# Reordering how the first right operands of a two-layer hybrid trunk are prepared on one Trainium2 core

## The chip, the cores and the metric

One core of a Trainium2 chip runs one program. The metric is device time in microseconds (us) of one execution. The engines are named as the profile names them: PE (TensorE matmuls), PEld (its weight loads), DVE (VectorE), ACT (ScalarE), POOL (GpSimd), SP (SyncE, which issues the DMA transfers here).

## The reference, cut to what matters

Two layers act on a latent stream `x` (512 tokens) and a context `s` (256 tokens), both of width 1024, float32. A layer is a half-step SwiGLU feed-forward (FFN), a token mixing (neighbourhood attention beside a two-way recurrent scan), and a second half-step FFN. The change touches only what precedes the first FFN of layer 0:

```python
mx = jnp.split((silu_c @ w_mod[l] + b_mod[l])[:, None, :], N_MOD, axis=-1)   # nine modulations; ms likewise
x = x + 0.5 * mx[2] * swiglu(modulate(rms_norm(x, norm_gain[l, 0]), mx[0], mx[1]), ffn_up[l, 0], ffn_down[l, 0])
# rms_norm: x * rsqrt(mean(x*x) + eps) * gain;  modulate: x * (1 + scale) + shift
# swiglu: (silu(gate) * up) @ w_down, with gate, up = split(x @ w_up)
```

## The kernel before

**Layout.** Both streams lie side by side, transposed: eight tiles `x[k]` of 128 channels by 768 tokens (512 latent, 256 context). A matrix product takes a 128x128 weight block on the left and a token block on the right. Every float32 operand is split in two, `hi` (rounded, made by ACT) and `lo` (the rest, made by DVE as source minus `hi`), and a product is the three matmuls hi·hi, hi·lo, lo·hi (`split`, line 201).

**The up projection.** `up` (line 372) computes each of 22 column blocks `f` of the FFN's first matrix by a Strassen-Winograd scheme: seven products instead of eight, each of four k-tiles with three matmuls, so 84 matmuls (line 394) in a block. The right operands are seven combinations of the four quarters of the scaled input. They are made once for an FFN and used by all 22 blocks. The norm's factor `rstd` is applied after the products; the shifts of the modulation ride along as four extra columns of products 2 to 6. The seven products of a block take the PSUM banks "a", "co", "g", "p", "g", "p", "g" in that order (there are two of "a", one of "co").

**Making the right operands.** `prep_wino(kt)` (line 258) handles the k-tiles `kt` and `kt+4`. It scales both into `xs0`, `xs1` (ACT, by `gs`, latent and context columns apart), splits the left half of each as products 0 and 1, makes two differences on POOL and splits product 5, makes one more on POOL, splits products 2, 3 and 4, makes the last difference on DVE and splits product 6. Then `squares` (line 223) adds x² of the two tiles into `acc`: ACT squares into a tile `sq`, DVE adds. So one k-tile pair has 4 scalings, 7 splits, 3 subtractions on POOL, 1 on DVE, 2 squares. In layer 0's first FFN the shifts are not known yet, so `shifts=False`: the four edge columns are copied away (`edge`, line 281), and `prep_shifts` fills the shift columns of products 2 to 6 later, k-tile by k-tile, 20 small splits.

**The start of the program** (`run`, line 1173): load and multiply modulation 1, which gives `gs`; load `x`; load the weights `raw` of block 0; then for each of four k: `prep_wino(k)` and one step of modulation 0 (`mod`, line 177: a 1 MB load and 8 x 4 matmuls in bank "g"); then `prep_shifts`. The FFN begins with `prep_end` (line 312): it reduces `acc` over channels on PE (`ssps`, bank "a"), takes the root on ACT and the reciprocal on DVE, spreads the result by PE (`rsps`, twice bank "a") and copies it to `rstd`. Fillers (modulations 2, 4 and 3, in bank "a") are emitted between the blocks.

**What sets the order.** Nothing is ordered by hand here. A planner (`schedule_with_timeline_sim=True`) gives each engine a fixed order: an instruction has a priority by its place in the program, and a later one that is ready in the planner's own timing goes ahead of an earlier one that is not. Tiles come from tags with a counted number of buffers (`TAGS`, line 60): "g3" has three, "q4" three, "z" three, "x" six. The split parts of the right operands borrow the buffers of many tags in the order of `PARTS` (line 65): the iterator `operand_parts` (line 247) hands out half tiles, 56 in all. `wq`, the split weights of products 0, 1, 3 and 5, also lives in "q4"; `acc` and `rstd` in "z"; `sq` and the FFN's work tiles `up_g`, `up_u` in "g3". The scaled `xs` lie in "x" for k = 0 to 2 and in "g3" for k = 3.

Of the kernel before, what the change touches and what calls it, by code (L numbers as in the profile page):

```python
# [11 lines left out]
AF = mybir.ActivationFunctionType  # L12
ALU = mybir.AluOpType
# [13 lines left out]
XH = T // 2 + 2  # L27
LAT, CTX = slice(0, NL), slice(NL, T)
# [27 lines left out]
def free_ap(ap, dims, offset=0):  # L56
    return bass.AP(tensor=ap.tensor, offset=ap.offset + offset, ap=[list(ap.ap[0])] + [list(d) for d in dims])
# [5 lines left out]


PARTS = ("st",) * 3 + ("k",) * 2 + ("sp",) * 8 + ("ob",) * 4 + ("q4",) + ("z",) * 2 + ("x",) * 6 + ("r",) * 2
PARTS_LAT = ("st",) + PARTS[3:]

BANKS = dict(g=2, ch=1, co=1, p=2, a=2)
# [29 lines left out]
def interleave(gen, filler):  # L98
    for n, _ in enumerate(gen):
        for _ in range(5 if n < 2 else 1):  # L100
            next(filler, None)
    for _ in filler:
        pass
# [6 lines left out]
class Net:  # L110
# [135 lines left out]

    def operand_parts(self):
        h = self.half(self.prep_ctx)
        for tag in PARTS if self.prep_ctx else PARTS_LAT:
            t = self.t(tag, "b", dt=F32R)  # L250
            for o in range(0, TAGS[tag][0] - h + 1, h):
                yield t[:, o:o + h]
# [2 lines left out]
    def half(ctx):  # L255
        return XH if ctx else NL // 2 + 2

    def prep_wino(self, kt, tag="g3", shifts=True):

        l, s = self.prep_key  # L260
        h = self.half(self.prep_ctx)
        n = h if shifts else h - 4
        x0, x1 = [self.t(tag, f"xs{i}", 2 * XH) for i in range(2)]
        for k, t in ((kt, x0), (kt + 4, x1)):
            for xs, j in ((LAT, 0), (CTX, 1))[:2 if self.prep_ctx else 1]:
                self.act(t[:, xs], self.x[k][:, xs], AF.Copy, scale=self.gs[l, s][:, k, j:j + 1])
            if shifts:
                self.act(t[:, 2 * h - 4:2 * h].rearrange("p (a c) -> p a c", a=2), free_ap(self.mods[l][:, 3 * s, k], [[0, 2], [1, 2]]), AF.Copy)
        a, b = slice(0, h), slice(h, 2 * h)

        def part(i, src):
            hi, lo = next(self.parts)[:, 0:h], next(self.parts)[:, 0:h]
            w = src.shape[-1]
            self.split(src, hi[:, 0:w], lo[:, 0:w])
            self.bs[i].append((hi, lo))

        part(0, x0[:, a])
        part(1, x1[:, a])
        if not shifts:
            for i, t in enumerate((x0, x1)):  # L280
                self.nc.gpsimd.tensor_copy(self.edge[:, i, kt], t[:, n:h])
            a, b = slice(0, n), slice(h, h + n)
        self.tt(x0[:, a], x0[:, b], x0[:, a], ALU.subtract, self.nc.gpsimd)
        self.tt(x0[:, b], x1[:, b], x0[:, b], ALU.subtract, self.nc.gpsimd)
        part(5, x1[:, b])
        self.tt(x1[:, b], x1[:, b], x0[:, a], ALU.subtract, self.nc.gpsimd)
        part(2, x1[:, b])
        part(3, x0[:, b])
        part(4, x0[:, a])
        self.tt(x1[:, a], x1[:, b], x1[:, a], ALU.subtract)  # L290
        part(6, x1[:, a])
        self.squares(kt)
        self.squares(kt + 4)

    def prep_shifts(self):

        l, s = self.prep_key
        h = self.half(self.prep_ctx)
        n = h - 4
        e0, e1 = [self.edge[:, i].rearrange("p k (a c) -> p k a c", a=2) for i in range(2)]  # L300
        s0, s1 = [free_ap(self.mods[l][:, 3 * s, k], [[2, 4], [0, 2], [1, 2]]) for k in (0, 4)]
        c = {i: self.ends[:, j].rearrange("p k (a c) -> p k a c", a=2) for j, i in enumerate((2, 3, 4, 6))}
        self.tt(c[4], s0, e0, ALU.subtract)
        self.tt(c[3], s1, s0, ALU.subtract)
        self.tt(c[2], s1, c[4], ALU.subtract)
        self.tt(c[6], c[2], e1, ALU.subtract)
        c[5] = s1
        for i in (2, 3, 4, 5, 6):
            for k in range(4):
                hi, lo = [t[:, n:h].rearrange("p (a c) -> p a c", a=2) for t in self.bs[i][k]]  # L310
                self.split(c[i][:, k], hi, lo)
# [861 lines left out]
    def run(self, out):  # L1173
        nc = self.nc
        self.x = [self.t("r", f"x{k}", T) for k in range(KD)]
        for _ in self.mod(0, 1, "st", SW, "a"):
            pass
        for k in range(4):
            for m in (k, k + 4):
                nc.sync.dma_start(out=self.x[m], in_=self.a["x"][:, m])  # L1180
        self.prep_begin(0, 0, True)
        edge = self.t("ro", "edge", 96).rearrange("p (i k n) -> p i k n", k=4, n=4)
        self.edge, self.ends = edge[:, 0:2], edge[:, 2:6]
        steps = self.mod(0, 0, "st", SW, "g")
        for k in range(4):
            self.prep_wino(k, "x" if k < 3 else "g3", False)
            next(steps, None)
        for _ in steps:
            pass
        self.prep_shifts()  # L1190
        mods = self.fillers([(0, i) for i in (2, 4, 3)], "ro", 256, "a")
        for l in range(L):
            last = l == L - 1
            self.xd = self.dp.tile([KD, 128, T], F32, name=f"xd{l}")

            def to_mix(m):
                if m == 0:
                    self.prep_begin(l, 1, True)
                for k in (m, m + 4):
                    self.prep(k)  # L1200
                    self.spill(k)

            def to_ffn(m):
                if m == 0:
                    self.prep_begin(l, 2, not last)
                self.prep_wino(m)

            def onward(m):
                if last:
                    for k in (m, m + 4):  # L1210
                        nc.sync.dma_start(out=out[:, k], in_=self.x[k][:, LAT])
                    return
                if m == 0:
                    self.prep_begin(l + 1, 0, True)
                self.prep_wino(m)

            interleave(self.ffn(l, 0, True, to_mix), mods)
            self.mix(l, last, to_ffn)
            interleave(self.ffn(l, 1, not last, onward), iter(()))
# [100 lines left out]
```

## Time and profile before

| | us |
|---|---|
| median of 3 runs | 3880.44 |
| the three runs | 3858.85, 3880.44, 3891.4 |
| the profiled execution | 3867.65 |
| its span, first to last instruction | 3865.8 |
| PE busy in the span | 3593.8 (93%) |
| DVE busy | 2918.1 (75%) |
| ACT busy | 1503.8 (39%) |
| POOL busy | 1078.3 (28%) |

The profile is of one execution, recorded by the hardware; its own time stands beside its span, and the difference is what lies around the span. The share of busy time is an average over stages with different limits. The busy time of DVE and POOL includes time in which an instruction has begun and is held up. The granted clock is the share of TensorE's full clock (2.4 GHz) that was granted; 0.5 is the lower of its two levels.

### The profile page before, as it was taken

How to read it: one execution, taken by the hardware profiler on the slowest of the kernel's cores; microseconds unless marked ns; L12 is line 12 of the kernel's file. 1: busy time of each engine (PE TensorE's matmuls, PEld its weight loads, DVE VectorE, ACT ScalarE, POOL GpSimd, SP SyncE). 2: the span in 40 equal slices, each digit the busy share in tenths (PEclk: the TensorE clock that was granted, in tenths of full speed). 3: DMA queues.
4: the chain of work that ended last, by engine and by line, in shares of the span. 5: the costliest groups of instructions: out<-in, count | busy, mean ns of one | idle time of the engine just before them, and what ended most of it. 6: DMA issues, size and time to landing. Idle time of an engine off the chain costs nothing. (4 is left out here: it accounts for less than half of the span.)

```text
span 3865.8 us, 73287 instructions
## 1 busy us (share of the span) xinstructions
PE 3593.8 (93%) x28980; PEld 3116.1 (81%) x28980; DVE 2918.1 (75%) x5612; ACT 1503.8 (39%) x2996; POOL 1078.3 (28%) x1208
## 2 busy tenths in 40 slices
PE   6999999999899899899998999999999996879999
PEld 4789998787665667799998999998786665768999
DVE  6578786666777776888888888886668677667878
ACT  5233334334343433433335333334434343244433
POOL 3222230202222211322233222230203123124665
PEclk9999999999798799899998999999999895789999
DMA  5321113322345263112211111213333431221232
GB/s 205 122 86 66 69 63 101 99 92 79 98 139 160 74 194 96 36 66 72 76 69 47 66 66 66 76 63 113 105 101 121 147 97 33 76 66 66 88 108 79
DMA packets 213943, 352.50 MB, mean 91 GB/s; under 512 B 46432, under 2 KB 128992, under 8 KB 201312
## 3 DMA queue, kind: packets, MB, share of 16 engines
q1 hardware_dynamic: 213600, 347.81, 27.7%
q8 instruction: 229, 3.75, 0.4%
q14 instruction: 114, 0.93, 0.1%
HBM read 305.26 MB, written 42.47 MB: 90 GB/s over the span
## 5 line engine op out<-in xcount | busy, mean ns | idle before, releaser
L394 PE MATMUL mw<-b,wq 128*128 128x386 f32 (+1 forms) x4224 | 788.6, 329 | 18.4 <-DVE wq L165 13.3
L394 PEld LDWEIGHTS mw<-b,wq 128*128 128x128 f32 x4224 | 705.0, 191 | 38.8 <-DVE wq L165 17.7
L352 PE MATMUL mm<-h,whi 128*128 128x256 f32 (+1 forms) x2816 | 650.1, 326 | 2.8 <-ACT h L171 1.8
L394 PE MATMUL mw<-b,whi 128*128 128x386 f32 (+1 forms) x2112 | 518.6, 328 | 14.9 <-DVE b L165 8.3
L168 DVE SCALAR_TENSOR_TENSOR x<-mm,mods,x 128x256 f32<-128x256 f32 (+1 forms) x704 | 390.7, 581 | 184.8 <-PE mm L352 181.3
L352 PEld LDWEIGHTS mm<-h,whi 128*128 128x128 f32 x2816 | 465.8, 188 | 58.4 <-issue 8.9
L352 PE MATMUL mm<-h,wlo 128*128 128x256 f32 (+1 forms) x1408 | 439.8, 325 | 2.0 <-DVE wlo L165 1.9
L394 PEld LDWEIGHTS mw<-b,whi 128*128 128x128 f32 x2112 | 374.3, 191 | 20.6 <-DVE b L165 10.5
L171 ACT ACTIVATE whi<-wraw 128x512 fp32r<-128x512 f32 x312 | 195.9, 629 | 490.1 <-PE mm L352 274.2
L165 DVE TENSOR_TENSOR wq<-raw,wq 128x512 fp32r<-128x512 f32 x352 | 312.8, 891 | 55.7 <-ACT wq L171 53.4
L394 PE MATMUL mw<-b,wlo 128*128 128x386 f32 (+1 forms) x1056 | 347.0, 329 | 3.6 <-DVE wlo L165 2.7
L171 ACT ACTIVATE wq<-raw 128x512 fp32r<-128x512 f32 x352 | 220.1, 629 | 303.7 <-PE mw L394 284.7
L352 PEld LDWEIGHTS mm<-h,wlo 128*128 128x128 f32 x1408 | 261.6, 188 | 27.9 <-DVE wlo L165 2.6
L165 DVE TENSOR_TENSOR up_g<-up_g,mw 128x386 f32<-128x386 f32 (+1 forms) x352 | 181.9, 517 | 78.8 <-PE mw L394 69.1
L165 POOL TENSOR_TENSOR raw<-raw,s 128x512 f32<-128x512 f32 x88 | 122.0, 1386 | 400.3 <-DVE wq L165 396.5
L165 DVE TENSOR_TENSOR wlo<-wraw,whi 128x512 fp32r<-128x512 f32 x268 | 186.3, 696 | 51.5 <-ACT whi L171 34.9
L171 ACT ACTIVATE whi<-s 128x512 fp32r<-128x512 f32 x176 | 110.1, 628 | 281.5 <-PE mm L352 199.2
L165 POOL TENSOR_TENSOR s<-raw 128x512 f32<-128x512 f32 x88 | 127.6, 1450 | 304.7 <-DVE wlo L165 293.9
L352 PE MATMUL mm<-x,whi 128*128 128x258 f32 (+2 forms) x832 | 209.2, 337 | 0.1
L394 PEld LDWEIGHTS mw<-b,wlo 128*128 128x128 f32 x1056 | 201.4, 191 | 7.6 <-DVE wlo L165 7.1
L165 POOL TENSOR_TENSOR up_g<-up_g,rstd 128x386 f32<-128x386 f32 (+1 forms) x88 | 107.0, 1216 | 346.6 <-DVE up_g L165 346.6
L188 PE MATMUL modps<-wmod,cs 128*32 128x256 f32 x1152 | 164.8, 443 | 28.1 <-DMA wmod<-in_w_mod_dram 27.3
(249 smaller groups left out, 7090.9 us busy)
## 6 DMA issues: line engine op xcount, KB each, us to landing
raw<-in_ffn_up_dram SPq DMA_DIRECT2D x88, 1024.0 KB, 5.2
wmod<-in_w_mod_dram SPq DMA_DIRECT2D x208, 256.0 KB, 3.0
wraw<-in_ffn_down_dram SPq DMA_DIRECT2D x176, 256.0 KB, 3.1
wraw<-in_w_in_dram SPq DMA_DIRECT2D x104, 256.0 KB, 2.9
wmod<-in_w_mod_dram SPq DMA_DIRECT2D x96, 128.0 KB, 2.3
wmod<-in_w_mod_dram SPq DMA_DIRECT2D x8, 1024.0 KB, 10.8
wraw<-in_w_out_dram SPq DMA_DIRECT2D x32, 256.0 KB, 3.1
in<-rkv SPq DMA_DIRECT2D x20, 384.0 KB, 3.7
```

Source lines behind the costliest of these rows:

```text
L165: (eng or self.nc.vector).tensor_tensor(out=out, in0=a, in1=b, op=op)
L168: self.nc.vector.scalar_tensor_tensor(out=out, in0=a, scalar=s, in1=b, op0=op0, op1=op1)
L171: self.nc.scalar.activation(out, in_, f, **kw)
L188: nc.tensor.matmul(ps[q:q + 32], lhsT=self.cs[:, kt], rhs=w, start=kt == 0, stop=kt == KD - 1)
L352: nc.tensor.matmul(ps, lhsT=wt, rhs=xt[k][:, c0:c1], start=k == 0 and n == 0, stop=k == nk - 1 and n == 2)
L394: nc.tensor.matmul(ps, lhsT=wt[:, c], rhs=self.bs[i][k][xt], start=k == 0 and m == 0, stop=k == 3 and m == 2)
```

## The change

The four calls of `prep_wino(k, ..., False)` are replaced by one new function, `prep_all`. It makes the same instructions on the same data, in another order of the program: all four k-tiles' latent scalings of the lower half, then product 0's four splits, the upper half's scalings, product 1's splits, all context scalings, the edge copies and the first two POOL differences of every k, product 5's splits, the third POOL difference of every k, the splits of products 2, 3 and 4, the DVE difference and product 6, and last the squares of all eight tiles. All steps of modulation 0 are emitted ahead of it, no longer one after each k-tile. `PARTS_ALL` has the same tags as `PARTS`, with "r" ahead of "x", since six `xs` now hold all of "x" at once. `prep_wino` loses its `shifts=False` branch; its other callers are unchanged.

```diff
+PARTS_ALL = PARTS[:20] + ("r",) * 2 + ("x",) * 6
@@ operand_parts
-        for tag in PARTS if self.prep_ctx else PARTS_LAT:
+        for tag in PARTS_ALL if self.prep_key == (0, 0) else PARTS if self.prep_ctx else PARTS_LAT:
@@
+    def prep_all(self):
+
+        l, s = self.prep_key
+        h = self.half(True)
+        n = h - 4
+        a, b, low = slice(0, h), slice(h, h + n), slice(0, n)
+        xs = [[self.t("x" if k < 3 else "g3", f"xs{i}", 2 * XH) for i in range(2)] for k in range(4)]
+        pool = self.nc.gpsimd
+
+        def scaled(i, cols, j):
+            for k in range(4):
+                m = k + 4 * i
+                self.act(xs[k][i][:, cols], self.x[m][:, cols], AF.Copy, scale=self.gs[l, s][:, m, j:j + 1])
+
+        def part(n, i, cols):
+            for k in range(4):
+                hi, lo = next(self.parts)[:, 0:h], next(self.parts)[:, 0:h]
+                w = cols.stop - cols.start
+                self.split(xs[k][i][:, cols], hi[:, 0:w], lo[:, 0:w])
+                self.bs[n].append((hi, lo))
+
+        scaled(0, LAT, 0)
+        part(0, 0, a)
+        scaled(1, LAT, 0)
+        part(1, 1, a)
+        for i in range(2):
+            scaled(i, CTX, 1)
+        for k in range(4):
+            x0, x1 = xs[k]
+            for i in range(2):
+                pool.tensor_copy(self.edge[:, i, k], xs[k][i][:, n:h])
+            self.tt(x0[:, low], x0[:, b], x0[:, low], ALU.subtract, pool)
+            self.tt(x0[:, b], x1[:, b], x0[:, b], ALU.subtract, pool)
+        part(5, 1, b)
+        for k in range(4):
+            x0, x1 = xs[k]
+            self.tt(x1[:, b], x1[:, b], x0[:, low], ALU.subtract, pool)
+        part(2, 1, b)
+        part(3, 0, b)
+        part(4, 0, low)
+        for k in range(4):
+            x1 = xs[k][1]
+            self.tt(x1[:, low], x1[:, b], x1[:, low], ALU.subtract)
+        part(6, 1, low)
+        for k in range(8):
+            self.squares(k)
@@ run
         steps = self.mod(0, 0, "st", SW, "g")
-        for k in range(4):
-            self.prep_wino(k, "x" if k < 3 else "g3", False)
-            next(steps, None)
         for _ in steps:
             pass
+        self.prep_all()
         self.prep_shifts()
```

## Rows read from the trace of the kernel before

**Rows 1.** Page, busy time: us (share of the span) x instructions.
```profile
PE 3593.8 (93%) x28980; PEld 3116.1 (81%) x28980; DVE 2918.1 (75%) x5612; ACT 1503.8 (39%) x2996; POOL 1078.3 (28%) x1208
```

**Rows 2.** Windows: length, busy (x count) per engine, PE clock, DMA share, GB/s.
```profile
20.00:70.00 50.00, 26.82 (x163) 19.20 (x164) 41.93 (x76) 32.99 (x81) 29.27 (x28) 0.83 0.50 189
70.00:76.00 6.00, 6.00 (x39) 5.15 (x38) 5.47 (x10) 2.68 (x5) 1.00 (x1) 1.00 0.34 97
76.00:108.00 32.00, 30.39 (x164) 22.39 (x162) 21.74 (x36) 11.57 (x20) 6.63 (x6) 1.00 0.55 172
```

**Rows 3.** Windows of line 394 alone: length, PE, PEld, PE clock, DMA share, GB/s.
```profile
20.00:63.78 43.78, 7.17 (x28) 5.94 (x29) 0.81 0.53 206
```

**Rows 4.** Timeline of DVE: start, us, engine line op out<-in xcount [idle before <-releaser].
```profile
19.12 0.96 DVE L165 TENSOR_TENSOR acc<-acc,sq 128x768 f32<-128x768 f32 x1 [0.32 <-ACT sq L171]
...
21.06 0.17 DVE L168 SCALAR_TENSOR_TENSOR gs<-mods,vecs 128x16 f32<-128x16 f32 x1
...
27.19 1.67 DVE L165 TENSOR_TENSOR acc<-acc,sq 128x768 f32<-128x768 f32 x1 [4.98 <-ACT sq L171]
...
30.23 6.54 DVE L165 TENSOR_TENSOR b<-xs,b 128x386 fp32r<-128x386 f32 x6
...
42.95 0.95 DVE L165 TENSOR_TENSOR acc<-acc,sq 128x768 f32<-128x768 f32 x1
...
57.00 0.16 DVE L165 TENSOR_TENSOR mods<-modpt,vecs 128x16 f32<-128x16 f32 x1
...
59.29 1.69 DVE L165 TENSOR_TENSOR b<-xs,b 128x386 fp32r<-128x386 f32 x2
...
68.32 1.01 DVE L165 TENSOR_TENSOR b<-xs,b 128x382 fp32r<-128x382 f32 x2
```

**Rows 5.** Tile view of the parts, 20 to 76 us: shortest/median/longest ns.
```profile
L165 DVE TENSOR_TENSOR b<-xs,b x28: 542/546/1642, 28.8 to 68.8; 128x382 fp32r<-128x382 f32 x20, 128x386 fp32r<-128x386 f32 x8
...
L171 ACT ACTIVATE b<-xs x28: 505/512/526, 27.1 to 67.3; 128x382 fp32r<-128x382 f32 x20, 128x386 fp32r<-128x386 f32 x8
```

**Rows 6.** Timeline of POOL.
```profile
26.79 1.26 POOL L165 TENSOR_TENSOR s<-raw 128x512 f32<-128x512 f32 x1 [0.51 <-DMA raw<-in_ffn_up_dram]
...
39.10 2.45 POOL L165 TENSOR_TENSOR xs<-xs,xs 128x382 f32<-128x382 f32 x2
47.25 1.58 POOL L165 TENSOR_TENSOR xs<-xs 128x382 f32<-128x382 f32 x1 [5.70 <-DVE b L165]
```

**Rows 7.** Timeline of ACT.
```profile
17.31 0.84 ACT L171 ACTIVATE acc<-x 128x768 f32<-128x768 f32 x1 [10.80 <-DMA x<-in_x_dram]
...
21.27 5.16 ACT L171 ACTIVATE xs<-x,gs 128x512 f32<-128x512 f32 x10 [0.20 <-DVE gs L168]
...
34.46 0.61 ACT L171 ACTIVATE whi<-s 128x512 fp32r<-128x512 f32 x1
...
46.65 1.28 ACT L171 ACT_TABLE_LOAD   x1
...
49.94 0.52 ACT L171 ACTIVATE b<-xs 128x382 fp32r<-128x382 f32 x1 [0.55 <-POOL xs L165]
...
51.31 1.13 ACT L171 ACTIVATE wq<-raw 128x512 fp32r<-128x512 f32 x2
...
54.80 0.85 ACT L171 ACTIVATE rstd<-rsps 128x512 f32<-128x512 f32 x2
...
63.78 0.47 ACT L171 ACTIVATE up_g<-mw 128x386 f32<-128x386 f32 x1
```

**Rows 8.** Timeline of PE.
```profile
44.05 2.69 PE L319 MATMUL ssps<-consts,acc 128*128 128x2 f32 x12 [9.61 <-DVE acc L165]
...
46.67 3.64 PE L188 MATMUL modps<-wmod,cs 128*32 128x256 f32 x32
...
50.24 2.11 PE L330 MATMUL rsps<-consts,rs 128*128 128x128 f32 x12
...
89.29 2.27 PE L394 MATMUL mw<-b,wq 128*128 128x386 f32 x12
```

More of the change, by code (lines that the diff above doesn't have):

```diff
@@ L256, in half, with prep_wino @@
         return XH if ctx else NL // 2 + 2
-    def prep_wino(self, kt, tag="g3", shifts=True):
+    def prep_wino(self, kt):
         l, s = self.prep_key
         h = self.half(self.prep_ctx)
-        n = h if shifts else h - 4
-        x0, x1 = [self.t(tag, f"xs{i}", 2 * XH) for i in range(2)]
+        x0, x1 = [self.t("g3", f"xs{i}", 2 * XH) for i in range(2)]
         for k, t in ((kt, x0), (kt + 4, x1)):
@@ L266, in prep_wino @@
                 self.act(t[:, xs], self.x[k][:, xs], AF.Copy, scale=self.gs[l, s][:, k, j:j + 1])
-            if shifts:
-                self.act(t[:, 2 * h - 4:2 * h].rearrange("p (a c) -> p a c", a=2), free_ap(self.mods[l][:, 3 * s, k], [[0, 2], [1, 2]]), AF.Copy)
+            self.act(t[:, 2 * h - 4:2 * h].rearrange("p (a c) -> p a c", a=2), free_ap(self.mods[l][:, 3 * s, k], [[0, 2], [1, 2]]), AF.Copy)
         a, b = slice(0, h), slice(h, 2 * h)
@@ L272, in part @@
             hi, lo = next(self.parts)[:, 0:h], next(self.parts)[:, 0:h]
-            w = src.shape[-1]
-            self.split(src, hi[:, 0:w], lo[:, 0:w])
+            self.split(src, hi, lo)
             self.bs[i].append((hi, lo))
@@ L278, in prep_wino @@
         part(1, x1[:, a])
[L279 to L282, printed above, removed]
         self.tt(x0[:, a], x0[:, b], x0[:, a], ALU.subtract, self.nc.gpsimd)
```

## Prediction

> **What bounds the kernel now.** The page's busy times come first: PE is busy 93% of the span [rows 1], so time is to be won where PE lacks work. The windows show such a place, the one that the change touches. Between 20 and 70 us PE is busy 26.82 of 50 us and DVE 41.93; from 70 to 76 PE is full; from 76 to 108 PE has 30.39 of 32 and DVE only 21.74 [rows 2]. So until about 70 us PE waits for operands that DVE finishes, and after that PE is the bound and DVE has 32 - 21.74 = 10.3 us of slack. Whatever PE can do ahead of 70 us comes off the end, as far as DVE can follow.
>
> The timeline of DVE tells why it takes so long. `gs` is written at 21.06; the `lo` of the last parts runs at 68.32 to 69.3; the ones of products 0 and 1 (386 columns) for the last k-tile run only at 59.29 [rows 4]. POOL stood 5.70 us before the third k-tile's differences, waiting for DVE [rows 6]. So the k-tiles go one after another, and every product of block 0 lacks its last k-tile until about 60 us. The windows of line 394 give the result: when product 0 is taken out of its bank (`up_g`, 63.78 [rows 7]) PE has done 28 of the block's 84 matmuls [rows 3].
>
> The second chain at the start is the norm. The last add of squares ends at 42.95 + 0.95 = 43.9 [rows 4]; `ssps` takes 2.69, 3.64 us of the modulation's matmuls follow, then `rsps` 2.11 [rows 8]; a table load of 1.28 lies between, and `rstd` is copied at 54.80 to 55.65 [rows 7]. Product 0 uses bank "a", which `ssps` and `rsps` take before it. So two chains end close together: parts at about 60, norm at about 56.
>
> **The change, part by part.** No instruction is removed or added: 16 scalings, 28 `hi`, 28 `lo`, 16 differences, 8 edge copies, 8 squares, 7 adds and modulation 0's loads and matmuls are all there. What changes is the order and who holds which buffer.
>
> *The two first products.* Ten scalings took 5.16 us [rows 7], 0.52 each; a `hi` takes 0.512 and an undisturbed `lo` 0.546 [rows 5]. By the new order ACT does 4 scalings and 4 `hi` by 21.3 + 8 x 0.52 = 25.4, 4 and 4 more by 29.6, the 8 context scalings by 33.7. With a `lo` behind each, product 0 is ready near 26 and product 1 near 30, not 61. This is the gain that the change can give.
>
> *POOL.* A k-tile's first difference takes 1.58, two others 2.45 together [rows 6]. They can start with the first context scaling, about 30.0. Four sets take 4 x (1.58 + 2.45) = 16 us, to about 46, where before the third set began at 47.25. Block 0's weight sums lie before them from 26.79 on, when `raw` lands.
>
> *DVE.* It has the same work, and two holes at the start: no `lo` before 23.9, none between 26.0 and 28.0, none between 30.1 and 34.1, together 2.7 + 2.0 + 4.0 = 8.7 us, against 50 - 41.93 = 8.1 us idle now [rows 2]. Three adds of squares (0.96 each, from 19.12 on [rows 4]) filled the time before `gs`, two of them ahead of it. If they move back, 1.9 us come in. So DVE ends the parts at 69.3 + 0.6 + 1.9 = 71.8, no earlier than now. If the squares still fill early holes, it ends 1.9 us sooner.
>
> *The squares and the buffers.* Here I read a rule of the planner out of the trace. The `hi` of `wq` (product 0) runs at 51.31, although `raw` is there since 26.79 [rows 6]; the `hi` of product 2's weights, later in the program, runs at 34.46. What separates them is the tag: "w2" is free, while "q4" is first asked for by parts 35 and 36, which for k = 2 are made at 49.94 [rows 7]. So buffers of a tag are given out in the order of the program. By that rule the new place of the squares costs more than priority. `acc` is the third request of "z", behind parts 37 to 40: product 3 of k = 2 and 3 and product 4 of k = 0. The POOL difference for k = 2 ends at 30.0 + 3 x (1.58 + 1.23) = 38.4, so `acc` comes near 41, where now it is made at 17.31 [rows 7]. And the seven `sq` come after two `xs` that hold two of the three "g3" buffers, so a square and its add alternate: 0.84 + 0.95 to 0.84 + 1.67 [rows 4, 7], seven times 12.5 to 17.6 us. The last add ends at 54.3 to 59.4, not 43.9.
>
> *The norm behind them.* From 43.9 to 55.65 it takes 11.7 us; without the modulation's 3.64 (done before, as the squares no longer stand in front of it) 8.1. So product 0 gets its bank at 62.4 to 67.5 and is taken out after 12 matmuls (2.27 [rows 8]) and 0.47: at 65.1 to 70.2, by 1.3 to 6.5 us later than 63.78. Queued behind are all adds of block 0 on DVE, since product 0 is the first term. PE is not held meanwhile: products 1 to 5 have banks "co", "g", "p", "g", "p" and their parts by about 50. So PE will have done 72 matmuls at that point, not 28: 44 x 0.18 (7.17 and 12 matmuls in 2.27 [rows 3, 8]) = 7.9 us ahead. The difference is a gain of 1.4 to 6.6; DVE's 2.5 us of delay fall into its slack of 10.3.
>
> *Modulation 0.* Ahead of the parts, its loads follow `raw` on SP as before. Its second half of matmuls stood behind `ssps` (46.67 [rows 8]), and its result came at 57.00 [rows 4]; now about 42. The shift columns of products 2 to 6 come sooner; it costs nothing, as all matmuls lie in PE's idle time. The range is 0 to 1 us for other load times.
>
> *"r" ahead of "x".* The last 11 parts reuse `xs` buffers as these die. The same engine that reads an `xs` writes the next part, so a wait of one split, 0 to 0.5 us.
>
> **Sum.** 7.9 ahead, less 1.3 to 6.5: I take the middle, 3.9, and a 1 us bound for loads and buffers off it: 3 us gain. The profiled execution is 3867.65 (span 3865.8 and 1.85 around it), so 3865 for it. It lies 12.8 below the median; the three runs and it have a mean of 3874.6. On that base the forecast is 3872.
>
> **Where a rule bears on it.** Six `lo` beside POOL's work took 6.54 us [rows 4], 1.09 each, twice the 0.546 of an undisturbed one [rows 5]. The Trainium skill (SBUF — State Buffer, "Who interferes with whom") says that a VectorE instruction with two SBUF inputs and a GpSimd one that reads SBUF share a read interface, and the second waits for the first. The trace agrees in the doubled time. It speaks against the change, because POOL's twelve differences now run in one piece beside DVE's splits.
>
> **The rivals.**
> 1. *Squares still early.* Should the planner not keep a tag's order, ACT squares from 17.31 as now, the norm is ready at 55.65, product 0 is out at 55.65 + 2.27 + 0.47 = 58.4, 5.4 sooner, and with 7.9 it would be 13.3, of which DVE's slack lets 10.3 through: 3864. Against it: the `wq` row.
> 2. *The norm becomes the bound (slower).* If the adds lie behind the last part on DVE, they end with it at 71.8. Then product 0 gets its bank at 79.9 and is out at 82.6, 18.9 later; less 7.9 it is 11 us slower: 3886. It decides from a last add ending at 60.8 (60.8 + 8.1 + 2.7 - 63.78 = 7.9). For it: squares have the lowest priority of the preparation. Against: POOL paces the parts, which leaves DVE holes in the plan.
> 3. *DVE and POOL in each other's way.* The 16 `lo` of products 5, 3, 4, 2 run beside POOL: 16 x 0.54 = 8.7 us extra, of which six (3.3) are paid already: 5.4 more, so 2 us slower than before: 3877.
> 4. *The plan of the rest shifts.* The planner lays out the whole program in time; a start moved by some us could change later choices by over 1%, 39 us. Nothing in the profile speaks for it, the rest being a fixed PE-bound sequence.
>
> **How the numbers follow.** Chances: forecast 0.48, squares early 0.20, norm the bound 0.20, DVE and POOL 0.07, plan 0.05. Forecast alone 3868 to 3875. All but the plan lie between 3864 and 3886; the runs before scatter by 16 to each side, so 3850 to 3893 holds 8 in 10. A measurement of this kernel tells about 1% from no change. All rivals but the last are below 0.4%: faster by over 1% 0.03, within 0.94, slower 0.03.
>
> **What would show it.** Right: `acc` first written after 38 us, one `sq` and one add in turn, `ssps` near 55 to 60, products 1 to 5 on PE from about 38, `up_g` between 65 and 70, modulation 0 near 42, the last `lo` near 70. Wrong: `acc` at 17 us, or `ssps` behind the last part, or PE still at 28 matmuls of line 394 when product 0 is taken out.

## The result, and the profile after

The changed kernel takes 3921.18 us (median of 5 runs, 3895.13 to 3941.62) against 3878.78 (5 runs of the kernel before beside it): ratio 1.011, 95% interval 1.0077 to 1.0144. It is slower by some 42 us; forecast were 3872 us and a range up to 3893. Its profiled execution took 3900.12 us, 32.5 more than that of before (3867.65). Helper lines are one higher in it (172 for ACT, 166 for DVE and POOL), later ones 41 (the product is line 435, `ssps` 360, `rsps` 371).

The page of the changed kernel, busy time:

```profile
PE 3604.9 (92%) x28980; PEld 3114.2 (80%) x28980; DVE 2910.3 (75%) x5612; ACT 1499.4 (38%) x2994; POOL 1075.8 (28%) x1208
```

Beside [rows 1], the work is the same (ACT has two instructions fewer) and PE's busy time is only 11.1 us longer; the rest of the 32.4 us of span is time in which PE stands. To see where it is lost, both spans are cut at the same marks: product 0 taken out (`up_g`), the norm of layer 0's mixing (the first FFN is left), and the end of that mixing (`rstd` of the next norm). Windows of the kernel before, columns as in [rows 2]:

```profile
0.00:63.80 63.80, 29.05 (x192) 16.43 (x193) 38.71 (x74) 33.77 (x78) 28.66 (x34) 0.87 0.65 249
63.80:625.60 561.80, 558.96 (x3138) 501.44 (x3137) 432.04 (x747) 194.32 (x349) 142.46 (x111) 1.00 0.27 88
625.60:1591.30 965.70, 867.49 (x8868) 665.23 (x8868) 671.67 (x1464) 390.92 (x842) 201.22 (x347) 0.89 0.35 107
```

The same windows of the changed kernel:

```profile
0.00:78.90 78.90, 36.23 (x232) 24.44 (x236) 41.59 (x88) 37.88 (x87) 29.14 (x34) 0.70 0.51 197
78.90:636.60 557.70, 555.03 (x3100) 495.48 (x3101) 424.14 (x732) 189.48 (x339) 142.15 (x111) 1.00 0.27 89
636.60:1621.80 985.20, 881.34 (x8869) 666.94 (x8869) 668.11 (x1464) 390.75 (x843) 202.03 (x347) 0.90 0.34 105
```

Product 0 comes out 15.1 us later; 4.1 of that are won back in the FFN, which is left 11.0 us later. Then the mixing stage of layer 0, whose code is untouched and whose instruction counts are equal to within one, takes 19.5 us more. The four stages behind it differ by 1.9 us in sum. So there are two losses, and the second lies where the prediction did not look.

**The start.** The timeline of ACT in the changed kernel, for [rows 7]:

```profile
20.39 2.13 ACT L172 ACTIVATE xs<-x,gs 128x512 f32<-128x512 f32 x4 [13.51 <-DVE gs L169]
...
41.01 0.83 ACT L172 ACTIVATE acc<-x 128x768 f32<-128x768 f32 x1
...
45.17 1.13 ACT L172 ACTIVATE wq<-raw 128x512 fp32r<-128x512 f32 x2
48.00 0.84 ACT L172 ACTIVATE sq<-x 128x768 f32<-128x768 f32 x1 [1.70 <-DVE acc L166]
...
61.06 0.61 ACT L172 ACTIVATE wq<-raw 128x512 fp32r<-128x512 f32 x1
...
75.84 0.87 ACT L172 ACTIVATE rstd<-rsps 128x512 f32<-128x512 f32 x2 [0.26 <-PE rsps L371]
78.94 0.49 ACT L172 ACTIVATE up_g<-mw 128x386 f32<-128x386 f32 x1 [2.23 <-PE mw L435]
```

ACT stands 13.51 us before `gs`, where it squared before. `acc` is first written at 41.01, not 17.31, and `wq` (the split weights of products 0, 1, 3, 5) comes at 45.17 twice and then only at 61.06. The timeline of DVE, for [rows 4]:

```profile
46.55 0.54 DVE L166 TENSOR_TENSOR xs<-xs 128x382 f32<-128x382 f32 x1
47.02 0.94 DVE L166 TENSOR_TENSOR acc<-acc,sq 128x768 f32<-128x768 f32 x1
47.89 0.54 DVE L166 TENSOR_TENSOR xs<-xs 128x382 f32<-128x382 f32 x1
48.36 5.15 DVE L166 TENSOR_TENSOR b<-xs,b 128x382 fp32r<-128x382 f32 x4
53.43 0.41 DVE L191 COPY modsb<-modps 128x256 f32<-128x256 f32 x1
53.76 1.28 DVE L166 TENSOR_TENSOR wq<-raw,wq 128x512 fp32r<-128x512 f32 x2
54.96 0.94 DVE L166 TENSOR_TENSOR acc<-acc,sq 128x768 f32<-128x768 f32 x1
...
57.85 0.16 DVE L166 TENSOR_TENSOR mods<-modpt,vecs 128x16 f32<-128x16 f32 x1
...
63.76 0.54 DVE L166 TENSOR_TENSOR b<-xs,b 128x382 fp32r<-128x382 f32 x1
...
65.68 0.94 DVE L166 TENSOR_TENSOR acc<-acc,sq 128x768 f32<-128x768 f32 x1
```

The last `lo` ends at 64.3, 5 us sooner than before. But the seventh add ends at 66.6 (43.9 before), and `modsb`, the `lo` of `wq` and the second add stand behind the `lo` of four splits, which take 5.15 us. PE shows who waits, for [rows 8]:

```profile
37.10 1.94 PE L189 MATMUL modps<-wmod,cs 128*32 128x256 f32 x16 [1.53 <-DMA wmod<-in_w_mod_dram]
46.35 1.01 PE L435 MATMUL mw<-b,wq 128*128 128x386 f32 x2 [7.31 <-ACT wq L172]
53.90 0.69 PE L194 MATMUL modpt<-consts,modsb 128*128 128x128 f32 x2 [6.53 <-DVE modsb L191]
55.09 3.58 PE L435 MATMUL mw<-b,wq 128*128 128x386 f32 x10 [0.51 <-DVE wq L166]
61.73 1.01 PE L435 MATMUL mw<-b,wq 128*128 128x386 f32 x2 [3.05 <-ACT wq L172]
...
67.32 2.18 PE L435 MATMUL mw<-b,wq 128*128 128x386 f32 x10
...
70.40 1.40 PE L360 MATMUL ssps<-consts,acc 128*128 128x2 f32 x12
...
74.75 1.50 PE L371 MATMUL rsps<-consts,rs 128*128 128x128 f32 x12
76.49 2.41 PE L435 MATMUL mw<-b,wq 128*128 128x386 f32 x12 [0.24 <-ACT rstd L172]
```

Until 60 us PE does product 1 and nothing else of the block: it stands 7.31 us for `wq`, 6.53 ahead of the transposes `modpt`, which wait for `modsb`, and 3.05 for the next `wq`. The transposes lie ahead of the products in its fixed order, but it is not they that hold product 1: its third matmul needs the `lo` of `wq`, which DVE makes from 53.76 to 55.04, and once the transposes are done PE waits another 0.51 us for it. Product 0 waits for its bank until `rstd` is copied. The windows of line 435, for [rows 3], say how far PE is at before's 63.78, and at 78.94:

```profile
20.00:63.78 43.78, 6.42 (x16) 4.91 (x17) 0.54 0.50 195
20.00:78.94 58.94, 18.86 (x72) 16.40 (x72) 0.62 0.38 147
```

The 72 matmuls of the forecast are reached only at 78.94, when product 0 is out; the kernel before has done 98 by then.

### The profile page after: what moved, and what is told of

It reads as the page before. It is cut to its first block, busy times and chain, and to the rows that moved or that the text cites. A ratio compares the mean times of both kernels' runs of the same rounds, so it can differ in the third digit from the quotient of the medians.

```text
span 3898.2 us, 73335 instructions
## 1 busy us (share of the span) xinstructions
PE 3604.9 (92%) x28980; PEld 3114.2 (80%) x28980; DVE 2910.3 (75%) x5612; ACT 1499.4 (38%) x2994; POOL 1075.8 (28%) x1208
## 5 line engine op out<-in xcount | busy, mean ns | idle before, releaser
L166 DVE TENSOR_TENSOR wq<-raw,wq 128x512 fp32r<-128x512 f32 x352 | 311.9, 888 | 63.7 <-ACT wq L172 60.7
```

Source lines behind the costliest of these rows:

```text
L166: (eng or self.nc.vector).tensor_tensor(out=out, in0=a, in1=b, op=op)
```

## The experiments

All kernels compute the whole result. A "root" is the instruction `sd` of `prep_end` (0.25 us on ACT), repeated with the same result to move the rest of the plan in time. "FFN left", "mixing 0" and "mixing 1" are the marks above in each one's profile, in us; ratios are against runs of the kernel before on the same chip.

| kernel | `up_g` | FFN left | mixing 0 | mixing 1 | ratio (95%) |
|---|---|---|---|---|---|
| before | 63.8 | 625.6 | 965.7 | 847.5 | |
| before again | 64.0 | 627.1 | 972.8 | 851.0 | 1.0009 (0.9984 to 1.0033) |
| changed | 78.9 | 636.6 | 985.2 | 848.0 | 1.0110 (1.0077 to 1.0144) |
| changed again | 77.3 | 634.6 | 981.6 | 858.9 | 1.0106 (1.0075 to 1.0137) |
| changed, squares first | 64.3 | 630.4 | 966.3 | 859.7 | 0.9990 (0.9972 to 1.0007) |
| changed + 12 roots | 82.3 | 640.1 | 964.3 | 867.7 | 1.0025 (1.0008 to 1.0042) |
| before + 8 roots | 63.7 | 628.6 | 970.9 | 838.6 | 0.9966 (0.9940 to 0.9992) |
| changed + 8 roots | 78.8 | 638.0 | 964.2 | 846.7 | 1.0003 (0.9983 to 1.0023) |
| before, squares last | 77.3 | 636.7 | 982.8 | 868.1 | 1.0087 (1.0061 to 1.0114) |
| before, modulation ahead | 63.2 | 625.2 | 992.4 | 855.5 | 1.0070 (1.0042 to 1.0098) |
| changed, norm in bank "p" | 64.0 | 622.3 | 986.6 | 861.0 | 1.0063 (1.0041 to 1.0085) |
| modulation ahead + 12 roots | 66.8 | 629.4 | 964.6 | 848.4 | 1.0018 (0.9992 to 1.0045) |
| bank "p" + 4 roots | 63.2 | 620.0 | 975.9 | 841.2 | 0.9999 (0.9977 to 1.0020) |
| changed + 14 roots | 81.5 | 638.1 | 974.0 | 848.2 | 1.0052 (1.0028 to 1.0076) |

The repeats of the same program set the scale: 7.1 and 3.6 us in mixing 0, 3.5 and 10.9 in mixing 1. How much of that goes with the granted clock is told below.

### The start

**Squares first.** On the changed kernel, the squares go back ahead of the parts:

```diff
+        for k in range(8):
+            self.squares(k)
         scaled(0, LAT, 0)
...
-        for k in range(8):
-            self.squares(k)
```

> The changed kernel with one part undone: the squares of all eight tiles come first in the new function instead of last; everything else stays product by product. The planned order after the start differs again; its first third of the mixing stage of layer 0 is that of the kernel before. Theory (norm behind the squares, plus another plan of the mixing stage): the last add of squares ends by about 45 us instead of 66.6, product 0 is taken out by 60 instead of 78.9 (63.8 before), and the first feed-forward stage is left 3 to 15 us earlier than in the changed kernel by that much, at 615 to 626 instead of 636.6 (625.6 before). Rival A (the product-by-product order itself delays the operands, by DVE and POOL in each other's way): product 0 is still taken out at 75 us or later and the stage is left near 636. For the mixing stage of layer 0 (965.7 us before, 985.2 in the changed kernel) the theory names no length, since the plan is a third one: 955 to 995; rival B (something in the changed order itself, such as the exchanged buffers, slows that stage) says 985 within 4.

Measured: `rstd` is copied at 50.36 and 51.49, product 0 comes out at 64.30, the FFN is left at 630.4, and the ratio is 0.9990. Its timelines of ACT and, of the matmuls, PE:

```profile
50.36 0.58 ACT L172 ACTIVATE rstd<-rsps 128x512 f32<-128x512 f32 x1
...
53.72 1.13 ACT L172 ACTIVATE wq<-raw 128x512 fp32r<-128x512 f32 x2
...
64.30 0.47 ACT L172 ACTIVATE up_g<-mw 128x386 f32<-128x386 f32 x1
...
64.68 1.38 ACT L172 ACTIVATE wq<-raw 128x512 fp32r<-128x512 f32 x2
```

```profile
54.39 1.01 PE L435 MATMUL mw<-b,wq 128*128 128x386 f32 x2 [2.10 <-ACT wq L172]
...
59.59 5.74 PE L435 MATMUL mw<-b,wq 128*128 128x386 f32 x20 [2.24 <-DVE wq L166]
```

So the late squares cause the late product 0. But product 0 was expected out by 60 and the FFN left by 626, and both missed: with the norm out of the way and products 0 and 1 long made, PE still starts them at 54.39, when the `hi` of `wq` is there, stands again for its `lo` before 59.59, and the next `wq` comes at 64.68. The order by products, which was to give the gain, gives none; it waits for the weights.

**Squares last alone.** On the kernel before, k-tile by k-tile as it was:

```diff
-        self.squares(kt)
-        self.squares(kt + 4)
+        if shifts:
+            self.squares(kt)
+            self.squares(kt + 4)
...
             next(steps, None)
+        for k in range(8):
+            self.squares(k)
```

> The kernel before with one part of the change alone: k-tile by k-tile as before, but the squares of all eight tiles stand after the fourth k-tile. Theory (the norm behind the squares sets the start): the last add of squares ends after 60 us (43.9 before), product 0 is taken out at 70 to 80 us (63.8 before, 78.9 changed), the first feed-forward stage is left 5 to 13 us later than 625.6. Rival A (the product-by-product order is what delays the start): product 0 taken out by 66, the stage left at 624 to 628. The mixing stage of layer 0 has another plan again: 955 to 990, no side named.

Measured: product 0 out at 77.25, FFN left at 636.7, ratio 1.0087. Its timeline of ACT, `rstd` and product 0:

```profile
74.17 0.87 ACT L171 ACTIVATE rstd<-rsps 128x512 f32<-128x512 f32 x2 [0.26 <-PE rsps L331]
...
77.25 0.49 ACT L171 ACTIVATE up_g<-mw 128x386 f32<-128x386 f32 x1 [2.21 <-PE mw L395]
```

The one part of the change gives all of the 11 us at the start.

**Modulation ahead alone.** On the kernel before:

```diff
-        steps = self.mod(0, 0, "st", SW, "g")
+        for _ in self.mod(0, 0, "st", SW, "g"):
+            pass
         for k in range(4):
             self.prep_wino(k, "x" if k < 3 else "g3", False)
-            next(steps, None)
```

> The kernel before with the other small part alone: all of modulation 0 is emitted ahead of the four k-tiles instead of one step after each. Theory: modulation 0 was never what the start waits for; product 0 taken out within 3 us of 63.8, first feed-forward stage left within 4 us of 625.6. Rival: the result of modulation 0 is held in DVE's and PE's fixed order in front of the products (in the changed kernel PE stood 6.53 us before the transposes), and the stage is left 5 us or more later. Mixing stage of layer 0: 955 to 990, no side named.

Measured: the FFN is left at 625.2, 0.4 us from before, so this part costs the start nothing, as forecast. Yet the kernel is slower, 1.0070, and mixing 0 takes 992.4, above the 955 to 990 that were expected. This separated the two losses; it is taken up below.

**The norm in another bank.** On the changed kernel, the norm of the first FFN gives product 0's bank free; the squares stay last:

```diff
-        ps = self.bank("a", "ssps", (128, nt, 2))
+        bank = "p" if self.prep_key == (0, 0) else "a"
+        ps = self.bank(bank, "ssps", (128, nt, 2))
...
-            pb = self.bank("a", "rsps")
+            pb = self.bank(bank, "rsps")
```

> The changed kernel with one edit: the first norm's sums and spread take PSUM bank p instead of a, so that product 0 does not ask for its bank behind them; the squares stay last. Theory (product 0 waits for the norm through the bank): product 0 is taken out at 64 to 70 us instead of 78.9 although rstd is no earlier than 72, and the first feed-forward stage is left at 624 to 632 instead of 636.6. Rival A (operands late by DVE and POOL): product 0 taken out no earlier than 75, stage left near 636. Mixing stage: 955 to 990.

Measured, in its timeline of ACT:

```profile
63.99 0.47 ACT L172 ACTIVATE up_g<-mw 128x386 f32<-128x386 f32 x1
...
77.03 0.87 ACT L172 ACTIVATE rstd<-rsps 128x512 f32<-128x512 f32 x2 [1.20 <-PE rsps L372]
```

`rstd` is no sooner than in the changed kernel (75.84), but product 0 is out 13 us ahead of it, and the FFN is left at 622.3, 14.3 us sooner than in the changed kernel and 3.3 sooner than before (624 to 632 were expected). So the path goes from the squares through bank "a": what keeps product 0 from 64 to 79 us in the changed kernel is its place and no operand. The ratio of 1.0063 is again more than the start explains; mixing 0 takes 986.6.

### The untouched stage

Two theories stood for mixing 0: that it runs otherwise because of where the start leaves the chip (clock, transfers), or that the planner, which lays out the whole program, has chosen another order for it. Compared in the traces, the instruction orders of DVE, ACT and POOL in the two kernels are the same in the later three FFNs and, but for a few places, in the first one behind the start; in both mixing stages they are not, though no line of these was edited (in mixing 0, 897 of DVE's 1464 places differ). Repeated roots shift the planner's times by some us, and the numbers of them were chosen so that pairs of kernels have the same order in mixing 0.

```diff
-        self.act(sd, ps[:, :, 0], AF.Sqrt, bias=self.eps(0))
+        for _ in range(N if self.prep_key == (0, 0) else 1):
+            self.act(sd, ps[:, :, 0], AF.Sqrt, bias=self.eps(0))
```

**Changed + 12 roots** (N = 13) has the order of "squares first" in mixing 0, and the start of the changed kernel with 3 us on top.

> The changed kernel, its code unchanged but for the square root of the first norm, which is taken 13 times instead of once with the same result: 12 more small ACT instructions of 0.27 us, about 3 us, in the chain of the first norm. The planned order of the start stays, that of the mixing stage of layer 0 becomes the same as in the run with the squares first. Theory: product 0 is taken out at about 82 us, the first feed-forward stage is left at about 639, and the mixing stage of layer 0 takes as long as in the run with the squares first, within 4 us, whatever its start. Rival B (the changed order itself slows the mixing stage): 985 within 4, as in the changed kernel.

Measured: the FFN is left at 640.1, 3.5 later than in the changed kernel, and still the ratio falls from 1.0110 to 1.0025, since mixing 0 takes 964.3, as in "squares first" (966.3).

**Before + 8 roots and changed + 8 roots** (N = 9) share one order of mixing 0.

> The kernel before, its code unchanged but for the square root of the first norm, which is taken 9 times instead of once with the same result: 8 more small ACT instructions, about 2 us. Nothing of the change is in it; the planned order of the mixing stages is another one. Theory (the mixing stage's length goes with the plan, and any shift of the start can draw another): product 0 taken out at about 65 us, first feed-forward stage left at about 627, the mixing stage of layer 0 off 965.7 by more than 4 us, to either side. Rival B (only the changed order slows the mixing stage): 965.7 within 4, and the total that of the kernel before plus 2.

> The changed kernel with the square root of the first norm taken 9 times. The planned order of its mixing stage of layer 0 is the same as that of the kernel before with 9 roots. Theory: the start as in the changed kernel plus 2 us (product 0 taken out near 81, first feed-forward stage left near 639), the mixing stage of layer 0 as long as in the kernel before with 9 roots, within 4 us. Rival B: 985 within 4, longer than that kernel's.

Measured: 970.9 and 964.2 in mixing 0, 6.7 apart where 4 were expected; ratios 0.9966 and 1.0003. That 970.9 is 5 us off the 965.7 of the kernel before shows nothing by itself, since this kernel's second execution took 972.8. The changed kernel with a start as late as its own (638.0) is no slower than before. And the kernel before with 2 us of useless work is faster by 0.34%.

**Modulation ahead + 12 roots** (N = 13) has the order of the kernel before in mixing 0, but for two neighbouring places of DVE.

> The kernel before with modulation 0 ahead, and the square root of the first norm taken 13 times: by that the planned order of layer 0's mixing stage becomes that of the kernel before, in every engine. Without the extra roots it took 992.4 us. Theory (the stage's length goes with its plan): 966 within 7, although the code differs from the slow one only by 3 us of roots; first feed-forward stage left at 626 to 630, total within 0.4% of the kernel before. Rival B (the moved modulation slows the mixing stage): 985 or more again.

Measured: 964.6 against 992.4 without the roots; ratio 1.0018 against 1.0070. Product 0 came at 66.8, 3.6 us later than without the roots, as these lie on the norm's path. The windows of mixing 0, first without and then with the roots:

```profile
625.20:1617.60 992.40, 883.30 (x8868) 674.24 (x8867) 666.71 (x1464) 393.76 (x844) 205.81 (x347) 0.88 0.33 104
```

```profile
629.40:1594.00 964.60, 866.35 (x8868) 663.78 (x8868) 672.47 (x1464) 391.24 (x843) 199.59 (x347) 0.89 0.34 107
```

The same count of instructions, 27.8 us apart. Of mixing 0, 238 us ran at the lower granted clock without the roots and 206 with them; by the estimate below that is some 10 of the 27.8.

**Bank "p" + 4 roots** (N = 5) has the order of the kernel before too.

> The changed order with the norm in bank p, and the root taken 5 times: its planned order of layer 0's mixing stage is that of the kernel before. Theory: first feed-forward stage left at 621 to 625 (622.3 with one root, 625.6 before), mixing stage 966 within 7 instead of 986.6, total 0 to 0.4% below the kernel before: the changed order is then no slower. Rival B: mixing stage 980 or more, total 0.4 to 0.8% above.

Measured: 975.9 against 986.6, ratio 0.9999 against 1.0063. The direction holds, but 966 within 7 was expected: 975.9 is 10 us above the profile of before at the same order. In this execution 241 us of mixing 0 ran at the lower granted clock, against 211 us in that of before, which by the estimate below is the whole difference. A start that is left 5.6 us sooner did not show as a gain in time.

**Before again and changed again**, with no edit:

> The kernel before itself once more, for how far a stage's length repeats. Theory: product 0 taken out at 63.8 within 1, first feed-forward stage left at 625.6 within 3, mixing stage of layer 0 965.7 within 7, mixing stage of layer 1 847.5 within 12 (its share of the lower clock differed by 32 us between the two executions of the changed kernel). Rival C (a mixing stage of 980 and more is chance of an execution, not of a plan) would let it come out at 975 to 990 here too.

> The changed kernel itself once more, for how far a stage's length repeats. Theory (the mixing stage's length goes with its plan): product 0 taken out at 78.9 within 1, first feed-forward stage left at 636.6 within 2, mixing stage of layer 0 again 985 within 8, and the total 0.8 to 1.4% above the kernel before. Rival C (the 985.2 was chance of one execution): the mixing stage 960 to 972, as in the four runs before.

Measured: 972.8 and 981.6 in mixing 0. Both differ from their first profiles by as much as a small effect (972.8 is just outside the 7 us expected, and product 0 of the changed kernel came 1.6 us sooner where 1 was expected); the two kernels' ranges (965.7 and 972.8; 985.2 and 981.6) do not meet.

**Changed + 14 roots** (N = 15) has the order of "modulation ahead" in mixing 0 behind the first part of that stage.

> The changed kernel with the root taken 15 times: its planned order of layer 0's mixing stage is the one of the run with modulation 0 ahead alone (992.4 us). Theory: mixing stage 990 within 7, so slower than the 964.3 with two roots less; first feed-forward stage left at 638 to 642; total 0.9 to 1.5% above the kernel before. Rival C (chance of an execution): 964 as with 12 roots more.

Measured: 974.0, not the 990 expected; ratio 1.0052. This is a miss. The lower clock carries a part of it (208 us of the stage in this execution, 238 in that of "modulation ahead", some 10 of the 18.4 us by the estimate below); the rest may lie in the first part of the stage, in which the orders differ, and that is not shown.

**The clock's share.** Four executions have the order of the kernel before in mixing 0: that kernel twice, "modulation ahead + 12 roots" and bank "p" + 4 roots. They spent 211, 232, 206 and 241 us of the stage at the lower granted clock and took 965.7, 972.8, 964.6 and 975.9 us: all four lie within 0.2 us of one line, which rises by 0.33 us for each us at the lower clock. As an estimate, the line may be laid under the other orders too. Above it lie the two executions of the changed kernel by 20.8 and 17.6 us, "modulation ahead" by 17.5, bank "p" by 13.7, "squares last" by 10.2, "changed + 14 roots" by 8.9 and the two kernels with 8 roots by 6.9 and 5.8; below it lie "squares first" by 1.0 and "changed + 12 roots" by 3.3. Executions of one order now agree within some 3 us, and the orders still differ by up to 24. So the stage's length goes with its order, and the clock explains most of what was left over. In mixing 1 the repeats run at much the same rate: 3.5 and 10.9 us more for 10 and 32 us more at the lower clock. This line was found after the runs and was not forecast.

**Where in the stage.** The tile view of `pt` (transposes of the attention's weights at line 608, and of the recurrent scan's read-out at line 1068; both 41 higher in the changed kernel, one higher with roots) gives first and last start. Before:

```profile
L608 PE MATMUL pt<-consts,scs x32: 272/327/476, 1090.4 to 1397.0; 128*128 128x128 f32 x32
L1068 PE MATMUL pt<-consts,o x16: 327/329/477, 1009.1 to 1486.1; 128*128 128x128 f32 x16
```

Changed:

```profile
L649 PE MATMUL pt<-consts,scs x32: 272/328/474, 1094.5 to 1435.1; 128*128 128x128 f32 x32
L1109 PE MATMUL pt<-consts,o x16: 272/328/476, 1023.1 to 1517.7; 128*128 128x128 f32 x16
```

Modulation ahead alone:

```profile
L608 PE MATMUL pt<-consts,scs x32: 272/327/476, 1086.3 to 1437.3; 128*128 128x128 f32 x32
L1068 PE MATMUL pt<-consts,o x16: 272/328/476, 1009.7 to 1520.5; 128*128 128x128 f32 x16
```

Modulation ahead + 12 roots:

```profile
L609 PE MATMUL pt<-consts,scs x32: 272/327/478, 1089.5 to 1396.0; 128*128 128x128 f32 x32
L1069 PE MATMUL pt<-consts,o x16: 327/329/476, 1008.2 to 1488.9; 128*128 128x128 f32 x16
```

Counted from each one's start of the stage (625.6, 636.6, 625.2, 629.4), the first of either kind lie within 8 us of each other. The last weight transpose lies at 771, 799, 812 and 767, the last read-out at 861, 881, 895 and 860, and the stage ends at 966, 985, 992 and 965. From the read-out to the end all take 97 to 105. So the loss arises in the attention and the read-out of the scan, which two orders place 20 to 40 us later, and what is behind them only inherits it. Which of the changed places does it I have not isolated.

## Why the prediction was wrong

**What was right.** By the tag rule `acc` was forecast near 41 and came at 41.01; square and add alternate as said up to the third add (from 58 us on ACT is one square ahead). POOL's sets were forecast to end at 46; on the changed kernel's timeline the last difference ends at 41.51 + 2.37 = 43.9. Product 0 was forecast to wait for its bank behind the norm, and bank "p" shows that it does. That modulation 0 ahead of the parts costs the start nothing held too (625.2 against 625.6).

**The term that failed first: PE's lead.** "PE is not held meanwhile: products 1 to 5 have banks ... and their parts by about 50. So PE will have done 72 matmuls at that point, not 28." I priced banks and right operands and left out the left ones. The row with `wq` at 51.31 [rows 7] was in my hands, and I used its rule for `acc`, `sq` and nothing else. "q4" has three buffers, one taken by parts; `wq` gets the other two at 45.17, and one of these holds product 0's weights, which wait for the bank. Products 1, 3 and 5 have to pass the other on: product 1's last matmuls end at 55.09 + 3.58 = 58.7 and the next `wq` is made at 61.06; product 3's end at 67.32 + 2.18 = 69.5 and the one behind it is made at 69.59. And product 1, begun at 46.35, goes on only at 55.09, when DVE has made the `lo` of its weights behind four splits. At 63.78 PE has done 16 matmuls, not 28 and not on the way to 72. The lead of 7.9 us was a lag. In "squares first", where no norm is in the way, PE stands for the same `wq`.

**The last add.** Forecast 54.3 to 59.4, measured 66.6. I let a square and its add follow each other without pause; in fact DVE's fixed order puts splits between the first of them. One such gap, from the add at 47.02 to the one at 54.96, holds the four `lo` in 5.15 us beside POOL's work, 1.29 each where an undisturbed one takes 0.546 [rows 5]. From the add to the copy of `rstd` it then took 76.7 - 66.6 = 10.1, not the 8.1 that I gave the norm, as `ssps` begins at 70.40, behind products that PE does ahead of it.

**Modulation 0.** Forecast 42, measured 57.85. Its matmuls were done at 37.10 + 1.94 = 39.0, as expected, but the copy `modsb` stands in DVE's order behind the same four splits, at 53.43; and the transposes are done only at 54.59. The products lose next to nothing by it, as the `lo` of `wq`, which they need, comes from the same engine behind the same splits at 55.04: the cost of nothing was right, the time was not.

**DVE's end.** Forecast 71.8, measured 64.3 for the last `lo`: it has no hole from 40 to 66. This made nothing faster, as the weights and the norm end later.

**The rivals.** The second rival, the norm as the bound, happened at the start. It was to decide from a last add ending at 60.8, and priced the loss at 11 us with product 0 out at 82.6; measured are a last add at 66.6, product 0 out at 78.94, and an FFN left 11.0 us later. The size agrees partly by chance: product 0 was 3.7 us sooner than priced, and the lead that I took off was not there. Against it I wrote that POOL leaves DVE holes; from 40 to 66 us there are none.

The third rival is not borne out. The 28 `lo` took 16.6 + 6.6 = 23.2 us in the changed kernel and 15.6 + 7.2 = 22.8 before (groups of DVE by form, 20 to 72 us). The Trainium skill (SBUF — State Buffer, "Who interferes with whom") has VectorE and GpSimd wait for each other at a shared read interface; the four splits at 1.29 us beside POOL agree with it. But the sum of such waits hardly changed: one piece of contention took the place of several.

The fourth rival happened on top, and here stands the costliest sentence: "Nothing in the profile speaks for it, the rest being a fixed PE-bound sequence." That sequence is fixed only within one build. And it isn't all PE-bound: the mixing stage has PE busy 867.49 of 965.70 us in its window. The sum had no term for the plan and the chances gave it 0.05; it made the larger of the two losses.

**How much each.** The pairs with one order of mixing 0 give the price of the change itself: 1.0025 - 0.9990 = 0.35% ("changed + 12 roots", "squares first") and 1.0003 - 0.9966 = 0.37% (8 roots each), some 14 us, of which 9.7 and 9.4 us are in the FFN's later end. The first pair differs by the place of the squares and the roots, the second by the whole change. By the intervals each of these two prices is uncertain by some 10 us. The runs' granted clocks narrow it: the 71 runs of the kernel before that stand beside the experiments fall on a line, 2.9 us longer for each 0.001 less of mean granted clock, with a scatter of 3.5 us. Taken to one clock by that line, which is an estimate, the two pairs differ by 8.8 and 9.2 us, so by the FFN's later end alone.

At one clock the changed kernel is 33 us above that line in its first five runs and 28 in "changed again". Some 10 of these are the start, and some 18 to 21, by the estimate above, are mixing 0 in the order that the planner chose. The rest of the 42 us between the medians goes with a lower granted clock (0.930 in the mean of the five runs, 0.933 in the 71 of the kernel before); whether the change or chance lowered it the runs do not tell. Mixing 1 has other orders too, but it differs by 10.9 us between two executions of one program, so nothing of the order is read from it.

No version beats both kernels for a reason that could be kept: the 0.9966 for 8 useless roots goes with a higher granted clock in those runs (0.937), and at one clock they are only 2.3 us below the line.

## What to carry to other kernels

A product needs its left operand, its right operand and its bank: before you count matmuls done ahead, list all three with the time at which each buffer comes free, and where a rule on buffers was read from one tile, apply it to every tile of that tag. A reduction that is moved last is off the path only if nothing shares a bank or a buffer with it. Where a planner orders the whole program, a shift of a few us can reorder stages that nobody touched; compare kernels over several harmless shifts, or by stages with the same instruction order, and set the time at the lower clock beside each, before a difference of 1% is credited to an edit.

## What the runs showed of the hardware

In the changed kernel PE's granted clock stayed low while its work was sparse:

```profile
40.00:66.00 26.00, 9.32 (x25) 7.42 (x26) 26.00 (x58) 13.60 (x40) 13.52 (x15) 0.50 0.06 18
66.00:68.00 2.00, 2.00 (x8) 2.00 (x8) 0.72 (x2) 0.64 (x1) 0.00 (x0) 0.53 0.24 66
68.00:79.00 11.00, 10.76 (x72) 10.29 (x74) 2.92 (x6) 4.38 (x8) 0.00 (x0) 1.00 0.01 1
```

PE is busy 9.32 of 26 us at the lower level (0.50, that is 1.2 GHz), and ten matmuls take 3.58 us at 55.09; once it is busy without a break, the grant goes to 1.00 near 68, and ten took 2.18 from 67.32 on. The kernel before has 0.69 from 40 to 63.8, where PE is busy 16.81 of 23.8 us. So here the stall of PE also made the matmuls around it slower, 0.36 us each and not 0.22, a price that the forecast (0.18 per matmul at any time) did not have. A small busy share alone does not tell the level: from 20 to 40 us the kernel before has PE busy 3.81 us at 0.94 in one execution, and 3.87 us at 0.50 in the other.

The time that one stage spends at the lower level is also not a constant of the program: 211 and 232 us of mixing 0 in two executions of the kernel before, and the stage 7.1 us longer in the second. I had taken a stage's length from one profile to be good to a few us; here it is good to about 10, and to about 3 once the time at the lower level is allowed for.
